# Query and key projections of three attention slots as seven block products instead of eight, in fp16, woven with attention; keys and values of two slots parked in HBM

## The chip, the cores and the metric

One Trainium2 chip, eight cores in two dies (cores 0 to 3 and 4 to 7), one program on all eight, each core with 1024 of the 8192 tokens. The metric is the device time of the slowest core in microseconds (us). Most fast executions of a kernel agree within 0.3%; some executions fall into a slower state in which the cores of one die are granted a lower clock (the kernel before, in one run: 2862.85 us, with a mean clock of 0.858 to 0.867 on cores 0 to 3 and 0.995 to 0.997 on the others). Every length of a stage below comes from a profiled execution whose eight cores were undisturbed, unless said.

Names: PE is the matrix engine, PEld its weight load, DVE the vector engine, ACT the scalar engine, POOL the general one, SP an engine that here issues transfers (`spdma`). SBUF holds the kernel's tiles, PSUM the results of its matmuls: the program declares it as eight banks of 128 x 512 fp32 (`psall`). DMA moves the weights and the parked tiles between HBM and SBUF.

## The reference, cut to what matters

A two-layer decoder trunk. Only the token mixer of the first layer is touched: dilated causal attention with 12 heads, in 3 groups by (window, dilation), 4 head slots each; a slot's three outputs are merged by their softmax denominators.

```python
ATTN_GROUPS = ((128, 1), (512, 4), (2048, 16))  # (window, dilation)

def _dilated_attention_mixer(h, positions, w_in):
    proj = h @ w_in                                # (B, S, 3*1536 + 512)
    q, k, v, q_mem = jnp.split(proj, [...], axis=-1)
    q = _partial_rotary(q..., positions)           # on 32 of the 128 head dims
    k = _partial_rotary(k..., positions)
    for g, (window, dilation) in enumerate(ATTN_GROUPS):
        o, l = _dilated_group(q[g], k[g], v[g], window, dilation)
    w = jax.nn.softmax(jnp.stack(lses, axis=0), axis=0)
    merged = jnp.einsum('gbsh,gbshd->bshd', w, jnp.stack(outs, axis=0))

# layer: x = x + concat([mix_out, mem_out]) @ w_out ; x = x + swiglu(rms_norm(x))
```

The tokens of a residue class (position modulo the dilation) form a subsequence, so queries and keys have to be regrouped by class somewhere between the projection and the scores.

## The kernel before

All instructions are declared as operations with what they read and write. A list scheduler then fixes the order on each engine ahead of time, from its own estimates of durations, and places the semaphores. `pe`, `act`, `dve`, `spdma` declare an operation; `bank(b)` is a PSUM bank, `PB(b)` its name for the dependencies.

The queries and keys of slot `s` are 6 column blocks (x = 0, 1 and u = 0 to 2) by two halves of tokens; each is 16 matmuls into one of two banks. The columns are permuted so that the 32 rotary rows of three heads share the block u = 0 and can be rotated at once.

```python
    OB = (0, 1)
    def qk_units(s):
        qk = QK[s % 2]
        def unit(x, u, th):
            def f():
                pc, c = divmod(x * 3 + u, 2)
                w = weights(("qk", s, pc), w0[W0_S + s * 3 + pc])
                b = nextbank(OB)
                proj(b, 512, [(lambda t, k=k: t.matmul(
                    bank(b), w[k * 256 + c * 128:k * 256 + c * 128 + 128], hT[k * TOK + th * 512:k * TOK + th * 512 + 512],
                    start=(k == 0), stop=(k == 15))) for k in range(16)], ...)
                # tile(i): the place of row i in QK, by residue class; st is the dilation
                if u == 0:
                    put[x, th] = rotary(b, 6 + th, 96)     # 3 DVE operations, 96 x 512
                    copy(2, 3, 1)                          # ACT, 32 rows
                    return
                copy(u - 1, None, 0)                       # ACT, 128 rows
                copy(2, 0, u + 1)                          # ACT, 32 rows
                put[x, th](u - 1, *tile(u - 1))            # DVE, 32 rotated rows
                if u == 2:
                    put[x, th](2, *tile(2))
```

The regrouping by class is a strided read, written in order:

```python
    def classes(ap, st):
        return ap if st == 1 else ap.rearrange("p (m r) -> p r m", r=st)

    def put(j, dst, dreg, st):                             # inside rotary
        dve(lambda v: v.tensor_tensor(out=dst[0:32], in0=classes(ta.ap[qs, 0:n], st), in1=classes(tb.ap[qs, 0:n], st), op=ALU.add), ...)

    def copy_rows(b, n, src, dst, dreg, to, st):
        if src is None:
            act(lambda a: a.copy(out=dst, in_=classes(bank(b)[:, 0:n], st)), [PB(b)], dreg, n)
        else:
            act(lambda a: a.copy(out=dst[32 * to:32 * to + 32], in_=classes(bank(b)[32 * src:32 * src + 32, 0:n], st)), [PB(b)], dreg, n)
```

A slot's attention is twelve batches: scores into bank 2 or 3, Exp on ACT, the mask on DVE, then values and denominators accumulated in banks 4 to 7. At its end ("the close") ACT takes Ln and Exp of the denominators and DVE multiplies. The slots and the output projection:

```python
    for s in range(4):
        ...
        attend(s)
        if s < 3:
            for f in qk_units(s + 1):
                f()

    def oproj0(t, j):          # 7 of 8 matmuls need only slots 0 to 2 and the memory heads
        for h in range(2):
            ks = ((4, 5, 6, 7, 0, 1, 2), (3,))[h]
            pe(mm[0:7] if h == 0 else mm[7:8], ...)
        add_x(b, t, j)
```

The softmax here doesn't subtract the row's maximum and nothing guards it: scores larger than these inputs give would overflow.

## Time and profile before

| | before |
|---|---|
| time, median of 3 runs | 2526.04 us (2524.78 to 2857.17) |
| first score of the memory heads ("start") | 347.2 us |
| from there to the last query or key product ("stage") | 162.1 us |
| from there to slot 3's result ("attn3") | 19.5 us |
| from there to the first matmul of the feed-forward ("oproj") | 59.45 us |
| from there to its first down projection ("ffn") | 535.4 us |
| the rest | 1393.6 us |

The start is the mean over the eight cores of one profiled execution, since its cores differ by up to 7 us (343.5 to 350.6 us here); the other stages are medians over the cores (so they need not add up exactly). The profiled core that the page shows is core 4. More views of it. First the whole stage as one row (window; busy us and count of PE, PEld, DVE, ACT, POOL; granted clock; DMA share; GB/s):

```profile
350.60:512.90 162.30, 159.76 (x1201) 86.10 (x1222) 80.74 (x132) 87.75 (x194) 4.75 (x9) 1.00 0.34 67
```

PE is idle 2.5 us of 162.3. The list of what PE waits for from 350 to 513 us (total us, times, longest):

```profile
PE psall L1094 <- DVE pm L1085: 1.1, 2, 0.7
PE psall L859 <- ACT QK L588: 0.3, 1, 0.3
```

And ACT's copies of query and key rows, by shape (count; busy us, mean ns; idle before and its releaser):

```profile
L588 ACT CAST QK<-psall 32x512 bf16<-32x512 f32 x35 | 20.1, 575 | 11.2 <-DVE t L572 10.2
L586 ACT CAST QK<-psall 128x512 bf16<-128x512 f32 x23 | 13.4, 583 | 35.2 <-PE psall L859 32.5 <-remote 2.7
```

Their mean is nearly the same for 32 and for 128 rows (575 and 583 ns) and, although most of them read every 4th, 8th or 16th element, no single one in the timeline is longer than 0.6 us.

### The profile page before, as it was taken

How to read it: one execution, taken by the hardware profiler on the slowest of the kernel's cores; microseconds unless marked ns; L12 is line 12 of the kernel's file. 1: busy time of each engine (PE TensorE's matmuls, PEld its weight loads, DVE VectorE, ACT ScalarE, POOL GpSimd, SP SyncE). 2: the span in 40 equal slices, each digit the busy share in tenths (PEclk: the TensorE clock that was granted, in tenths of full speed). 3: DMA queues.
4: the chain of work that ended last, by engine and by line, in shares of the span. 5: the costliest groups of instructions: out<-in, count | busy, mean ns of one | idle time of the engine just before them, and what ended most of it. 6: DMA issues, size and time to landing. Idle time of an engine off the chain costs nothing.

```text
span 2524.4 us, 38262 instructions; the slowest of 8 cores (2512.0 to 2524.4 us)
## 1 busy us (share of the span) xinstructions
PE 2459.5 (97%) x13993; PEld 1305.3 (52%) x14059; DVE 1549.7 (61%) x2716; ACT 839.9 (33%) x1464; POOL 148.7 (6%) x250
## 2 busy tenths in 40 slices
PE   7999999989999999999999999999999999999998
PEld 3454445544456666644444764444566666544443
DVE  4761425556456677657777766336676776567767
ACT  6762245454223333320003444134333333310004
POOL 1100000000000000000000000000000000000003
PEclk9999999999999999999999999999999999999999
DMA  9865754364876655797652443524756555786554
GB/s 160 130 102 84 138 102 78 68 184 94 184 128 136 126 104 112 139 212 155 132 126 52 84 85 77 106 73 88 167 103 140 115 106 115 183 189 133 126 132 150
DMA packets 73431, 310.28 MB, mean 123 GB/s; under 512 B 6688, under 2 KB 34848, under 8 KB 47520
## 3 DMA queue, kind: packets, MB, share of 16 engines
q0 software_dynamic: 37344, 218.36, 49.9%
q1 hardware_dynamic: 35904, 89.47, 10.3%
q8 instruction: 115, 1.88, 0.3%
q14 instruction: 68, 0.56, 0.1%
HBM read 482.65 MB, written 43.52 MB: 208 GB/s over the span
## 4 chain that ended last, share of the span: by engine, by line
PE 88%; DMA 4%; ACT 2%; DVE 2%; issue 2%; another core or an unknown queue 0%; POOL 0%; DVEq 0%; ACTq 0%; POOLq 0%
PE psall L1471 28%; PE psall L1678 20%; PE psall L1413 11%; PE psall L859 6%; PE psall L2127 4%; PE psall L2033 4%; PE psall L812 3%; PE psall L1873 3%; PE psall L775 2%; PE psall L1253 2%; PE psall L739 2%; DMA stg<-xT 1%; PE psall L896 1%; DMA fr<-wgu 1%; DMA b_B<-wd 1%
## 5 line engine op out<-in xcount | busy, mean ns | idle before, releaser
L1167 DVE TENSOR_TENSOR xs<-psall,xs 128x512 f32<-128x512 f32 x400 | 270.2, 687 | 210.0 <-PE psall L1678 134.5
L1471 PE MATMUL psall<-Sq,ft 128*128 128x512 f16 x1408 | 323.5, 379 | 0.0
L1678 PE MATMUL psall<-b_B,units 128*128 128x512 f16 x1408 | 315.4, 380 | 4.1 <-DMA b_B<-wd 2.9
L1477 ACT COPY snap<-psall 128x512 f32<-128x512 f32 x264 | 151.5, 586 | 299.4 <-PE psall L1471 222.6
L1678 PE MATMUL psall<-b_T,units 128*128 128x512 f16 x1056 | 237.4, 379 | 1.7 <-DVE xs L1167 1.0
L1678 PEld LDWEIGHTS psall<-b_B,units 128*128 128x128 f16 x1408 | 137.7, 98 | 171.0 <-issue 7.9
L1471 PE MATMUL psall<-hTq,ft 128*128 128x512 f16 x912 | 212.1, 381 | 2.3 <-DVE hTq L1243 2.3
L1471 PEld LDWEIGHTS psall<-Sq,ft 128*128 128x128 f16 x1408 | 137.4, 98 | 147.1 <-issue 0.8
L1173 ACT ACTIVATE junkB<-xs 128x1024 bf16<-128x1024 f32 x24 | 25.3, 1054 | 464.1 <-DVE xs L1167 463.0
L859 PE MATMUL psall<-hT,ring 128*128 128x512 bf16 x741 | 169.8, 379 | 2.2 <-ACT QK L588 0.8
L1678 PEld LDWEIGHTS psall<-b_T,units 128*128 128x128 f16 x1056 | 102.9, 98 | 126.1 <-issue 3.1
L1471 PE MATMUL psall<-Sq,fr 128*128 128x512 f16 x704 | 159.8, 379 | 0.3 <-DVE snap L1516 0.2
L1471 PEld LDWEIGHTS psall<-hTq,ft 128*128 128x128 f16 x912 | 89.5, 98 | 99.6 <-issue 4.4
L1516 DVE TENSOR_TENSOR snap<-psall,snap 128x512 f32<-128x512 f32 x88 | 60.4, 686 | 115.3 <-PE psall L1471 115.3
L859 PEld LDWEIGHTS psall<-hT,ring 128*128 128x128 bf16 x768 | 73.6, 98 | 84.5 <-issue 4.4
L2127 PE MATMUL psall<-ring,G 128*128 128x512 f16 x512 | 111.8, 379 | 1.4 <-DVE G L2057 1.4
L1471 PEld LDWEIGHTS psall<-Sq,fr 128*128 128x128 f16 x704 | 68.3, 98 | 83.3 <-issue 3.6
L1361 DVE TENSOR_TENSOR ft<-fr 128x2048 f16<-128x2048 f16 x88 | 106.8, 1216 | 4.7 <-DMA fr<-wgu 4.7
L1413 PE MATMUL psall<-a2f,t2w 128*128 128x256 f16 x744 | 106.4, 272 | 0.3 <-DVE psall L1429 0.2
L1335 POOL DMA_DIRECT2D fr<-wgu x88 | 46.5, 529 | 1016.3 <-PE psall L1471 813.6
L1482 ACT ACTIVATE sgb<-psall 128x512 f16<-128x512 f32 x88 | 52.4, 595 | 139.9 <-PE psall L1471 135.2
L1422 ACT COPY psall<-psall 128x512 f32<-128x512 f32 x93 | 53.2, 572 | 135.4 <-PE psall L1413 135.4
(255 smaller groups left out, 3728.5 us busy)
## 6 DMA issues: line engine op xcount, KB each, us to landing
fr<-wgu POOLq DMA_DIRECT2D x88, 1024.0 KB, 13.3
ring<-w POOLq DMA_DIRECT2D x38, 1024.0 KB, 9.9
b_B<-wd POOLq DMA_DIRECT2D x32, 896.0 KB, 10.9
hid<-fs SPq DMA_DIRECT2D x44, 512.0 KB, 10.5
b_B<-wd POOLq DMA_DIRECT2D x16, 1024.0 KB, 14.5
units<-hid SPq DMA_DIRECT2D x16, 896.0 KB, 8.1
ring<-wo POOLq DMA_DIRECT2D x12, 1024.0 KB, 9.4
stg<-xT POOLq DMA_DIRECT2D x20, 512.0 KB, 16.7
```

Source lines behind the costliest of these rows:

```text
L812: pe([(lambda t, k=k, hf=hf: t.matmul(bank(b), own_tile(hT[k * TOK:(k + 1) * TOK], gi, j), ws[hf][(k % 8) * 512:(k % 8 + 1) * 512], start= ...
L859: proj(b, 512, [(lambda t, k=k: t.matmul(bank(b), w[k * 256 + c * 128:k * 256 + c * 128 + 128], hT[k * TOK + th * 512:k * TOK + th * 512 + ...
L1167: dve(lambda v: v.tensor_tensor(out=xa, in0=bank(b), in1=xa, op=ALU.add), [PB(b), xr], [xr], 512)
L1361: dve(lambda v: v.tensor_tensor(out=T[0:2048], in0=w[1024:3072], in1=w[0:2048], op=ALU.subtract), [w.r(0, 3072)], [T.r(0, 2048)], 2048, 2)
L1413: pe([(lambda t, k=k: t.matmul(bank(b)[:, h * 256:(h + 1) * 256], W[:, k * 128:(k + 1) * 128], g_(k), start=(first and k == 0), stop=False ...
L1471: pe([(lambda t, k=k: t.matmul(bank(b), W[blk * 1024 + k * 128:blk * 1024 + k * 128 + 128], f(k), start=(first and k == 0), stop=(last and ...
L1477: act(lambda a: a.copy(out=s_.ap, in_=bank(b)), [PB(b)], [s_.r()], 512)
L1516: dve(lambda v: v.tensor_tensor(out=s7.ap, in0=bank(X), in1=s7.ap, op=ALU.add), [PB(X), s7.r()], [s7.r()], 512)
L1678: pe([(lambda t, k=k: t.matmul(bank(b), f(u, k), w[k * 512:(k + 1) * 512], start=(first and k == 0), stop=(last and k == hG - 1), skip_gro ...
L1873: pe([(lambda e, k=k, i=i, t=t: e.matmul(bank(b)[:, i * 256:(i + 1) * 256], f(k, t), w(k), start=(first and i == 0 and k == 0), stop=(last ...
L2033: pe([(lambda t, k=k: t.matmul(bank(b), W[blk * 1024 + k * 128:blk * 1024 + k * 128 + 128], f(k), start=(first and k == 0), stop=(last and ...
L2127: pe([(lambda t_, k=k, hh=hh, hf=hf: t_.matmul(bank(b), G1[t * 2048 + (hh * 8 + k) * 128:t * 2048 + (hh * 8 + k) * 128 + 128], ws[hh][k * ...
```

## The change

The intent: multiply the 2 x 2 blocks of activations and weights with seven products instead of eight (Winograd's form of Strassen's scheme), as the feed-forward of this kernel already does, for slots 1 to 3. That needs sums of activation blocks (made in place, once), sums of weight blocks (per piece of 256 columns), and PSUM results that are partly copied out ("snapshots", fp32, in SBUF) and added to later results. The operands become fp16. To make room, halo keys and values of slots 2 and 3 and the values of two slots wait in HBM and come back when slots 0 and 1 are done. Attention batches are woven between the products, and part of the output projection is put early into slot 3's attention.

```diff
@@ the source of the copies and of rotary is now a parameter: a bank or a snapshot
-    def copy_rows(b, n, src, dst, dreg, to, st):
+    def copy_rows(ap, sr, n, src, dst, dreg, to, st):
         if src is None:
-            act(lambda a: a.copy(out=dst, in_=classes(bank(b)[:, 0:n], st)), [PB(b)], dreg, n)
+            act(lambda a: a.copy(out=dst, in_=classes(ap[:, 0:n], st)), [sr], dreg, n)
@@ seven products
+    def qk_piece(s, pc, out):
+        X, Y = OB[pc_i[0] % 2], OB[1 - pc_i[0] % 2]
+        def sums():                  # T1, T2, T4: one 128x2048, two 128x1024 on DVE
+            ...
+        def snapshot(key, b):
+            s_ = st[key] = snq[sq2_i[0] % 5]
+            act(lambda a: a.copy(out=s_.ap, in_=bank(b)), [PB(b)], [s_.r()], 512)
+        def done(c, th, b, key=None):
+            x, u = divmod(pc * 2 + c, 3)
+            if key is None:
+                out(x, u, th, bank(b), PB(b))
+            else:
+                s_ = st[key]
+                dve(lambda v: v.tensor_tensor(out=s_.ap, in0=bank(b), in1=s_.ap, op=ALU.add), ...)
+                out(x, u, th, s_.ap, s_.r())
+        def f1(): prod(X, True, 0, A(0, 0), True, False);  snapshot("s1", X)
+        def f2(): prod(Y, True, 3, A(1, 0), True, True);   done(0, 0, Y, "s1")
+        def f3(): prod(X, False, 2, S(1), False, False);   snapshot("s2", X)
+        def f4(): prod(Y, False, 1, A(0, 1), True, False); snapshot("s7", Y)
+        def f5(): prod(X, False, 0, S(0), False, False);   done(1, 1, X, "s7")
+        def f6(): prod(Y, False, 3, A(1, 1), False, True); done(0, 1, Y, "s2")
+        def f7(): prod(X, True, 2, S(2), False, True);     done(1, 0, X)
@@ parking, ahead of the memory keys
+    spdma(lambda q: q.dma_start(out=kvx, in_=KVh[4 * HALO:8 * HALO]), ...)       # 2.75 MB
+    spdma(lambda q: q.dma_start(out=vox, in_=Vo[6144:12288]), ...)               # 1.57 MB
@@ weaving
-        attend(s)
+        parts, close = attend(s)
         if s < 3:
-            for f in qk_units(s + 1):
-                f()
+            todo = ...               # three pieces of seven products, and their weight sums
+            interleave(todo, parts)
+        else:
+            run(parts)
+        close()
+        if s < 2:
+            ...                      # bring back what was parked
@@ output projection
+    EARLY = [(0, 0), (0, 1), (4, 0), (4, 1), (1, 0)]
+    for t, j in EARLY:
+        oproj0(t, j, (4, 5, 6, 7, 0, 1, 2), OB)
```

Left out: the buffers, the place of each weight piece, the order of weight columns on the host, the sums of activations, and the same change of parameter in `rotary`.

## The prediction

Its sum: -15.5 + 4 + 2 + 1 - 1.5 = -10 us, from 2526 to 2516, shaded to 2515. The 1 us of parking and the 3 us of the wait for an output weight, part of the -1.5, are estimates.

> **What bounds the kernel now.** I read the page's busy shares, then the table by stage, then the timeline of the matrix engine between 350 and 600 us, and last the tables for DMA. Busy shares of the page:
>
> ```profile
> PE 2459.5 (97%) x13993; PEld 1305.3 (52%) x14059; DVE 1549.7 (61%) x2716; ACT 839.9 (33%) x1464; POOL 148.7 (6%) x250
> ```
>
> PE is the bound over the whole span. The change touches the first 600 us, so what counts is whether PE is the bound there. Table by stage (us; busy of PE, PEld, DVE, ACT, POOL; granted clock; DMA share; GB/s):
>
> ```profile
> 350.00:400.00 50.00, 49.63 (x383) 27.09 (x389) 24.68 (x43) 36.30 (x80) 1.58 (x3) 1.00 0.28 52
> 400.00:450.00 50.00, 49.20 (x379) 26.71 (x385) 25.68 (x43) 23.78 (x55) 2.11 (x4) 1.00 0.45 84
> 450.00:500.00 50.00, 48.68 (x375) 26.35 (x381) 24.96 (x41) 23.43 (x54) 1.06 (x2) 1.00 0.36 72
> ```
>
> From 350 to 500 us (memory attention, attention of slots 0 to 2, query and key products of slots 1 to 3) PE is 98% busy, DVE half, DMA a third. A matmul less there is time less, and DVE seems to have 25 us free in 50. The groups of instructions between 340 and 600 us give the work and its prices:
>
> ```profile
> L859 PE MATMUL psall<-hT,ring 128*128 128x512 bf16 x554 | 127.9, 379 | 1.4 <-ACT QK L588 0.3
> L579 DVE TENSOR_TENSOR QK<-t,t 32x512 bf16<-32x512 f32 x36 | 35.6, 988 | 38.7 <-ACT QK L586 38.4
> L1085 DVE TENSOR_TENSOR pm<-pt,masks 128x512 bf16<-128x512 bf16 x48 | 19.8, 422 | 23.0 <-ACT pt L1079 19.2 <-PE psall L1096 3.4
> L571 DVE STREAM_SHUFFLE t<-psall 96x512 f32<-96x512 f32 x12 | 8.7, 728 | 0.1
> ```
>
> The projection matmul (554 records of 576) waits 1.4 us in all. Its 379 ns is a latency; the pitch is in the timeline of PE:
>
> ```profile
> 302.23 13.98 PE L859 MATMUL psall<-hT,ring 128*128 128x512 bf16 x62
> 316.04 13.98 PE L896 MATMUL psall<-hT,ring 128*128 128x512 bf16 x63
> ```
>
> The 64 matmuls of a block (62 recorded) take 316.04 - 302.23 = 13.81 us, 0.2158 us each. After the products attention of slot 3 stands alone; table by stage:
>
> ```profile
> 515.00:520.00 5.00, 4.32 (x52) 2.78 (x51) 2.62 (x5) 2.06 (x6) 0.53 (x1) 1.00 0.60 206
> 520.00:525.00 5.00, 3.40 (x71) 2.70 (x66) 1.20 (x3) 4.56 (x19) 0.00 (x0) 1.00 0.94 185
> 525.00:530.00 5.00, 4.53 (x62) 2.84 (x62) 0.92 (x3) 0.70 (x2) 0.00 (x0) 1.00 0.23 84
> 530.00:535.00 5.00, 1.46 (x4) 0.48 (x5) 2.09 (x3) 1.98 (x2) 0.53 (x1) 0.87 1.00 324
> 535.00:540.00 5.00, 4.78 (x19) 2.09 (x20) 2.17 (x5) 4.06 (x9) 0.00 (x0) 0.78 1.07 279
> ```
>
> From 515 to 535 us PE is idle 0.68 + 1.60 + 0.47 + 3.54 = 6.3 us, and DMA becomes full. And one earlier place, where DMA is the limit already:
>
> ```profile
> 265.00:270.00 5.00, 5.00 (x25) 2.25 (x23) 0.00 (x0) 0.58 (x1) 0.53 (x1) 1.00 0.98 172
> 270.00:275.00 5.00, 3.80 (x17) 1.40 (x15) 3.72 (x8) 1.16 (x2) 0.00 (x0) 1.00 1.02 241
> 275.00:280.00 5.00, 3.75 (x26) 2.54 (x27) 0.00 (x0) 0.40 (x2) 0.00 (x0) 1.00 1.03 175
> ```
>
> There PE loses 2.5 us, 1.9 of it to weights of the memory keys.
>
> [...] the fp16 feed-forward matmuls show the same 379 ns. [...] 128x2048 fp16 takes 1216 ns, 128x1024 683 ns, 128x512 with a PSUM operand 687 ns. [...]
>
> **The change part by part.**
>
> *Products.* A slot has 2 token halves x 6 column blocks x 16 contraction blocks = 192 matmuls; as seven products, 3 pieces x 7 x 8 = 168. Three slots save 72 x 0.2158 = 15.5 us of PE, on the path.
>
> *Sums.* Prices from the feed-forward, which does the same: own sums 8 x 1.216 = 9.7 us; weight sums 9 x (1.216 + 2 x 0.683) = 23.2; additions to a snapshot 27 x 0.687 = 18.5: DVE gains 51.4 us. ACT gains 27 snapshots x 0.586 = 15.8, harmless. Rotary now mostly reads SBUF instead of PSUM[...] (676 and 679 ns): no change.
>
> Is DVE still hidden? Per slot before: 12 x 0.984 + 4 x (0.728 + 0.676 + 0.679) + 12 x 0.422 + 1.22 = 26.4 us. The change adds 7.7 + 6.2: 40.3. PE per slot: 36.3 of products and, by columns, 36 x 0.2158 = 7.8 of attention: 44.0. By durations DVE would be 92% full. Operations back to back start about 0.07 us earlier than durations say (a 0.68 us one followed after 0.60), 55 x 0.07 = 3.9 us, so some 36.4, 83%. Six of the eight own sums are placed before the memory attention, when DVE idles. PE stays the bound, narrowly.
>
> *Two banks.* Seven products of 8 matmuls (1.73 us each) alternate between two PSUM banks, and five times per piece the next but one product needs a bank that ACT or DVE has just read: DVE for second, fifth and sixth product. DVE has 1.73 us, plus some 0.4 us of attention, for an operation of 0.69 us behind whatever of up to 1.2 us is running. At 83% load I put 0.15 us on each of the 27 DVE hand-overs: 4 us back. This is judged, not measured.
>
> *Start.* The place of a piece's weights changes, and the first piece now loads last of three, at a point where DMA is full; one sum over the activations and the first weight sums can only start when the last memory query product is done. 2 us back.
>
> *Parking.* 2.75 MB of keys and values and 1.57 MB of values go out at about 260 to 285 us, and as much comes back, after slots 0 and 1. The return lies where the DMA share is 0.28 to 0.45: free. The way out meets full DMA[...]. The instruction order moves the memory keys' matmuls later (64 projection matmuls before them now, 40 before), which hides part. 1 us back.
>
> *Tail.* Before, four partial output projections of 7 matmuls fill the lone attention of slot 3; the instruction order now shows seven, 3 x 1.5 = 4.5 us of the 6.3 idle. But one output weight, loaded long ahead before, now shares full DMA with another and with 2 MB of residual rows; the last two partials need those and stand ahead of the last attention products in PE's order. 9.4 us is the median for one alone[...]. I put 3 us on that wait: net -1.5.
>
> Everything later is untouched. Sum: -15.5 + 4 + 2 + 1 - 1.5 = -10 us. From 2526: 2516, which I shade to 2515.
>
> **The rivals.** *Full gain:* no new waits and a filled tail, -15.5 - 4.5 = -20, 2506. For it: DVE stands at half, and the feed-forward runs the same scheme at PE 98% or more. Against it: that has six banks, not two, and no attention in between. *DVE becomes the bound:* if operations overlap less than I take, or its fixed order puts 2.8 us of rotary ahead of an addition for which PE waits, a slot takes 47 to 49 us rather than 44; almost all of 49.3 is back, and the time is 2522 to 2527. For it: 92% by durations. Against it: the order shows additions between rotary steps. *DMA takes the gain:* parking delays memory and query weights before 350 us, and the two output weights hold PE at the tail; each could cost 5 us more: 2525. For it: a share of 1.0 in both places. Against it: the loads are ordered early and the stage before 350 has slack between 280 and 300 us.
>
> **Range and chances.** Full gain is the floor, DVE as the bound near the ceiling; I give the middle most: 2508 to 2525, 8 in 10. 2% is 50 us; the change reaches only 160 us and saves 15 of them at best, so "within 2%" is close to certain. Slower by 2% would need a stall of 60 us; nothing suggests one, but reordering could bring one.
>
> **What would show it.** Products right: 504 matmuls of this kind instead of 576, pitch still 0.216. DVE: about 40 us per 50 in that stage, and PE waits for snapshot additions or copies of 3 to 6 us in all; under 1 us means full gain, over 10 DVE as the bound. Start: PE idle by about 2 us around 350 to 357. Parking: PE waits for weights between 260 and 350 us of no more than 4 us. Tail: idle of PE between the last product and the final output projection below 6 us, with a wait for an output weight. Everything after must keep its length within 1 us. Wrong would be: a stage from 350 us to slot 3's attention that shortens by under 5 or over 15 us, or a changed clock with fp16 activations.

## The result, and the profile after

| | before | after |
|---|---|---|
| median | 2525.41 us (2524.46 to 2857.17, 4 runs) | 2523.28 us (2522.22 to 2585.27, 4 runs) |
| ratio | | 0.9991, 95% 0.9972 to 1.0011 |

A ratio is the mean time of one kernel's fast runs over that of the other's of the same rounds, so it is not quite the ratio of the medians. The change is correct. By the run times alone it is not told from no change, since the interval holds 1; by the stages it is worth about 2 us, where 10 were forecast: inside the range of the prediction, but its sum was wrong. Where it went, by stage (the start and the last row are means over the cores, the others medians):

| stage | before | after | difference | forecast |
|---|---|---|---|---|
| start | 347.2 | 349.3 | +2.1 | +3 (start and parking) |
| stage | 162.1 | 158.1 | -4.0 | -15.5 + 4 = -11.5 |
| attn3 | 19.5 | 23.9 | +4.4 | } -1.5 |
| oproj | 59.45 | 55.75 | -3.7 | } |
| ffn | 535.4 | 535.55 | +0.15 | 0 |
| rest | 1393.6 | 1394.0 | +0.4 | 0 |
| first matmul of the feed-forward, mean | 588.7 | 586.7 | -2.0 | |

The last row agrees with the medians of the run times, so the answer lies in the first 590 us. The page's profiled core of the kernel after is core 1; below I use core 4 of the same execution, as before (its span is 2513.4 us, the longest of the eight 2520.6: its start came earlier, its stages have the lengths of the others).

Page, busy shares (core 1):

```profile
PE 2450.1 (97%) x13987; PEld 1297.9 (51%) x13987; DVE 1599.5 (63%) x2783; ACT 873.8 (35%) x1491; POOL 148.7 (6%) x250
```

PE's work went down by 9.4 us, DVE's up by 49.8 and ACT's by 33.9. Table by stage of core 4, the three 50-us windows of the prediction and then the stage as one row:

```profile
350.00:400.00 50.00, 48.35 (x353) 25.54 (x351) 34.52 (x59) 41.60 (x83) 1.06 (x2) 1.00 0.24 44
400.00:450.00 50.00, 45.98 (x380) 24.66 (x379) 37.42 (x60) 34.42 (x62) 1.58 (x3) 1.00 0.47 109
450.00:500.00 50.00, 45.69 (x348) 23.80 (x347) 37.71 (x60) 34.75 (x63) 2.11 (x4) 1.00 0.56 131
```

```profile
346.30:504.60 158.30, 147.23 (x1137) 77.62 (x1136) 115.49 (x183) 117.86 (x218) 4.75 (x9) 1.00 0.43 95
```

PE is busy 12.5 us less and idle 11.1 instead of 2.5 us. (Why 12.5, when the products alone save 15.5: by its columns at the pitch of 0.216 us the stage holds some 158.8 us of matmuls before and 142.7 after, an estimate. The busy times show 1.0 and 4.5 us more than that: a matmul shows 379 ns where the pitch is 216, and so can hide short waits behind it; no run separated them.) DVE, the suspect of the prediction, has 36.5 us of work per 50, less than the 40 it reckoned with. ACT has 30.1 us more, twice the 15.8 it reckoned with. What PE waits for in the stage:

```profile
PE psall L947 <- DVE snq L962: 3.0, 2, 1.6
PE psall L947 <- ACT QK L592: 2.7, 5, 1.1
PE psall L1173 <- ACT pt L1188: 2.2, 3, 0.9
PE psall L947 <- ACT snq L954: 1.2, 2, 0.7
PE psall L1125 <- ACT pt L1123: 1.1, 2, 0.9
PE psall L1173 <- DVE QK L583: 0.8, 1, 0.8
```

L947 is a product, L1173 a score of a slot. Three of the four largest are ACT's. The copies of L592 that end the waits of products read PSUM, since a copy from SBUF frees no bank; in the timeline four of the five stand directly behind slow copies in ACT's fixed order (at 410 us behind two of 1.14 and 1.15 us). Its groups in the stage:

```profile
L592 ACT CAST QK<-snq 32x512 bf16<-32x512 f32 x27 | 29.4, 1090 | 11.6 <-DVE snq L962 11.1
L590 ACT CAST QK<-snq 128x512 bf16<-128x512 f32 x18 | 17.0, 947 | 14.7 <-DVE snq L962 14.7
L954 ACT COPY snq<-psall 128x512 f32<-128x512 f32 x27 | 15.9, 588 | 6.3 <-PE psall L947 6.0
...
L592 ACT CAST QK<-psall 32x512 bf16<-32x512 f32 x9 | 5.2, 575 | 1.0 <-DVE t L576 0.8
```

The snapshots (L954) cost what was forecast, 15.9 us. The rest is a copy that no one added: 45 row copies, 39 of them with a stride, now read a sum in SBUF (`snq`) instead of a bank, and the same 32x512 copy that takes 575 ns from PSUM takes 1090 ns from there. In the 128-row group the mean mixes two kinds: in the timeline, those without a stride take 0.61 to 0.68 us and those with one 1.06 to 1.14.

How a late ACT copy becomes idle PE shows in one gap, 403 to 408 us. Timelines of ACT, DVE and PE (start us, length us, engine, instruction; in brackets the idle time before it and what ended it):

```profile
402.90 1.08 ACT L590 CAST QK<-snq 128x512 bf16<-128x512 f32 x1
404.01 1.11 ACT L592 CAST QK<-snq 32x512 bf16<-32x512 f32 x1
```

```profile
404.08 2.21 DVE L583 TENSOR_TENSOR QK<-t,t 32x512 bf16<-32x512 f32 x2 [0.50 <-ACT QK L590]
406.31 0.69 DVE L962 TENSOR_TENSOR snq<-psall,snq 128x512 f32<-128x512 f32 x1
```

```profile
403.65 1.03 PE L947 MATMUL psall<-Sa,ring 128*128 128x512 f16 x4
404.52 0.38 PE L1173 MATMUL psall<-QK 128*128 128x256 bf16 x2
404.74 1.03 PE L947 MATMUL psall<-Sa,ring 128*128 128x512 f16 x4
407.14 1.89 PE L947 MATMUL psall<-hT,ring 128*128 128x512 f16 x8 [1.38 <-DVE snq L962]
```

ACT's strided copy ends at 403.98. DVE's put, which fills rows of the same tile, waited 0.50 us for it; the addition that frees the bank stands behind two puts in DVE's fixed order and ends at 407.0; PE, whose next product needs that bank, waits 1.38 us. The copy explains 0.50 of it; the two puts, 2.21 us, were there before the change. The first two PE rows also give the pitch: four products in 404.52 - 403.65 = 0.87 us, 0.217 each, as before.

The start: the PE waits of core 4 from 200 to 346 us contain one for the last weight piece of slot 0's queries and keys, where before there was 1.9 us for memory keys' weights:

```profile
PE psall L899 <- DMA ring<-w: 3.2, 1, 3.2
```

The tail, table by stage and timeline of PE:

```profile
505.00:510.00 5.00, 2.51 (x18) 1.23 (x17) 4.91 (x6) 4.92 (x7) 0.00 (x0) 0.80 0.73 211
510.00:515.00 5.00, 5.00 (x49) 3.29 (x48) 3.23 (x6) 1.48 (x5) 0.53 (x1) 0.86 0.49 75
...
525.00:530.00 5.00, 2.77 (x28) 1.36 (x27) 1.23 (x1) 2.08 (x2) 0.00 (x0) 1.00 1.01 415
```

```profile
507.69 0.19 PE L1203 MATMUL psall<-pm,KVh 128*128 128x64 bf16 x1 [2.49 <-DVE attnT L1255]
```

The filling works: PE is full from 510 to 525 (the rows left out read 5.00 too). Most of attn3's +4.4 us is this filling itself: 49 matmuls of partial output projections in place of 28, an estimate of 4.5 us at the pitch, work that oproj then lacks. So attn3 and oproj are best read together, +0.7. But a new wait of 2.5 us stands ahead of it: slot 3's first value matmul overwrites the accumulators of slot 2, which are free only when slot 2's close is done. The multiplication that ends slot 2's close, in the timeline of DVE before and after:

```profile
481.09 1.22 DVE L1142 TENSOR_TENSOR attnT<-psall,rden 128x1024 bf16<-128x1024 f32 x1 [3.36 <-ACT rden L1139]
```

```profile
506.33 1.21 DVE L1255 TENSOR_TENSOR attnT<-psall,rden 128x1024 bf16<-128x1024 f32 x1
```

Before, it came 32 us ahead of the last product (512.9) and was hidden; woven over all of the products, it comes 1.7 us after the last one (504.6). Behind the wait stands something that the prediction had no term for: the rows of 505 to 515 us show a granted clock of 0.80 and 0.86, and the first partial output projection after the wait takes 3.17 us where the next one, of as many matmuls, takes 1.67 (core 4).

### The profile page after: what moved, and what is told of

It reads as the page before. It is cut to its first block, busy times and chain, and to the rows that moved or that the text cites. A ratio compares the mean times of both kernels' runs of the same rounds, so it can differ in the third digit from the quotient of the medians.

```text
span 2520.6 us, 38404 instructions; the slowest of 8 cores (2512.6 to 2520.6 us)
## 1 busy us (share of the span) xinstructions
PE 2450.1 (97%) x13987; PEld 1297.9 (51%) x13987; DVE 1599.5 (63%) x2783; ACT 873.8 (35%) x1491; POOL 148.7 (6%) x250
## 4 chain that ended last, share of the span: by engine, by line
PE 86%; DMA 5%; DVE 3%; ACT 3%; issue 2%; POOL 0%; DVEq 0%; ACTq 0%; POOLq 0%
PE psall L1605 29%; PE psall L1812 20%; PE psall L1547 11%; PE psall L2261 4%; PE psall L2167 4%; PE psall L947 3%; PE psall L2007 3%; PE psall L816 2%; PE psall L1383 2%; PE psall L779 2%; DMA ring<-w 1%; DMA hT<-xT 1%; PE psall L743 1%; PE psall L899 1%; PE psall L1000 1%
## 5 line engine op out<-in xcount | busy, mean ns | idle before, releaser
L1568 DVE TENSOR_TENSOR psall<-psall,s5b 128x256 f32<-128x256 f32 x93 | 40.2, 433 | 88.1 <-PE psall L1547 88.1
L1605 PE MATMUL psall<-hTq,fr 128*128 128x512 f16 x416 | 93.2, 380 | 2.0 <-DVE upb L1637 1.0
```

The source lines that it names most:

```text
L1605: pe([(lambda t, k=k: t.matmul(bank(b), W[blk * 1024 + k * 128:blk * 1024 + k * 128 + 128], f(k), start=(first and k == 0), stop=(last and ...
```

## The experiments

Theories for the missing time, which the runs were chosen to tell apart: (A) ACT's row copies from SBUF are slow and hold up the chain; (B) two banks for seven products are too few; (C) DVE's own added work is; (D) parking or the load order delays the start; (E) weaving costs, by the exposed close. Eighteen kernels ran. Stages, in us. "Sum" is stage + attn3 + oproj. The start and the last column are means over the cores, the others medians.

| kernel | start | stage | attn3 | oproj | sum | first ffn matmul |
|---|---|---|---|---|---|---|
| before | 347.2 | 162.1 | 19.5 | 59.45 | 241.05 | 588.7 |
| after | 349.3 | 158.1 | 23.9 | 55.75 | 237.75 | 586.7 |
| e1_plain_copies | 349.5 | 152.8 | 22.9 | 55.75 | 231.45 | 581.0 |
| e2_no_weave | 349.0 | 165.6 | 21.5 | 56.95 | 244.05 | 592.9 |
| e3_close_early | 351.1 | 158.4 | 21.5 | 56.65 | 236.55 | 587.8 |
| e4_park_only | 346.4 | 162.1 | 19.5 | 59.45 | 241.05 | 587.7 |
| e5_early_off (disturbed) | 354.7 | 158.1 | 23.4 | 61.15 | 242.65 | 597.9 |
| e6_third_bank | 348.9 | 151.0 | 27.05 | 55.5 | 233.55 | 583.0 |
| e7_third_inplace | 349.5 | 150.5 | 26.8 | 55.5 | 232.8 | 582.4 |
| e8_best | 349.4 | 158.0 | 24.55 | 55.9 | 238.45 | 587.9 |
| e9_load_order | 348.6 | 160.2 | 23.9 | 55.25 | 239.35 | 587.6 |
| e10_fp16_only | 346.5 | 162.1 | 19.45 | 60.35 | 241.9 | 588.1 |
| e11_strided_write | 349.0 | 206.7 | 27.8 | 55.9 | 290.4 | 638.8 |
| e12_write_and_puts | 348.8 | 216.85 | 31.6 | 55.5 | 303.95 | 653.5 |
| e13_late_park | 347.1 | 158.0 | 24.0 | 55.7 | 237.7 | 584.3 |
| e14_no_weight_sums | 350.5 | 156.1 | 28.6 | 55.15 | 239.85 | 589.9 |
| e15_combined | 347.4 | 153.4 | 23.35 | 56.35 | 233.1 | 581.1 |
| e16_plain_third | 349.9 | 146.3 | 26.75 | 55.5 | 228.55 | 578.2 |
| e17_third_late | 348.4 | 150.5 | 26.85 | 55.5 | 232.85 | 581.2 |
| e18_all_psum | 348.0 | 151.0 | 25.6 | 54.1 | 230.7 | 578.8 |

### A: the copies

**e1_plain_copies.** Wrong result: row copies from SBUF read their source in order. Nothing else changes, not even the order of instructions, because the scheduler's estimate of a copy doesn't depend on its stride.

```diff
     def copy_rows(ap, sr, n, src, dst, dreg, to, st):
+        if sr[0] == "S" and st > 1:      # source in SBUF
+            ... in_=ap[:, 0:n].rearrange("p (r m) -> p r m", r=st) ...   # same shape, in order
+            return
```

> Changed kernel, but the row copies that read a sum in SBUF read it in order instead of regrouped by class (wrong result on purpose; same instructions in the same order). In the changed kernel these copies take 1.09 us on ACT against 0.58 us from PSUM. If the slow copies are what holds the matrix engine (they hold ACT, and DVE waits for them before it frees a bank), they fall to about 0.6 us, idle of PE between the first memory score and the last product falls from 11 us to under 6, and that stage from 158.1 us to 151 to 154. If it is the two banks and DVE's load, the stage stays within 157 to 158.5 although the copies are faster.

ACT's groups from SBUF in this run:

```profile
L592 ACT CAST QK<-snq 32x512 bf16<-32x512 f32 x27 | 16.6, 616 | 13.1 <-DVE snq L968 12.6
```

1090 ns became 616. The stage went from 158.1 to 152.8, and the sum fell by 6.3 us; the runs agree: 2518.75 us (2515.74 to 2563.22), ratio to before 0.9975 (0.9953 to 0.9997). Theory A is shown: the stride of the copies alone costs 6.3 us of the sum (5.7 at the first feed-forward matmul).

**e11_strided_write and e12_write_and_puts.** The obvious remedy: read in order and put the stride on the write side, for ACT's copies (e11) and for DVE's puts as well (e12). Both correct.

```diff
+        if sr[0] == "S" and st > 1:
+            i_, o_ = ap.rearrange("p (m r) -> p m r", r=st), dst.rearrange("p r m -> p m r")
+            act(lambda a: a.copy(out=o_, in_=i_), [sr], dreg, n)      # the 32-row case is left out
+            return
```

> Changed kernel, but the row copies from SBUF sums walk the sum in order and write the bf16 rows with the stride, in place of reading with the stride and writing in order; result stays correct. If reading fp32 with a stride from SBUF is what doubles the copy (1.09 us), it falls to 0.6 to 0.7 us, the stage from 158.1 to about 153 us as in the run with plain copies, and the total by 5 to 6 us. If any strided SBUF access costs the same, copies stay at 1.05 us or more and the stage at 158.

> As the previous kernel, and the 36 rotary additions on DVE (0.98 us mean, 1.05 strided, 0.68 in order) write with the stride too. If the write stride is free on DVE also, they fall to 0.68 us, DVE in the stage from 116 to about 106 us, and the stage by up to another 1 to 3 us (150 to 153). If not, no change against the previous kernel.

A clear miss. ACT's copies in e11, then DVE's puts in e12:

```profile
L594 ACT CAST QK<-snq 32x512 bf16<-32x512 f32 x19 | 47.2, 2482 | 9.9 <-DVE snq L970 9.5
```

```profile
L586 DVE TENSOR_TENSOR QK<-t,t 32x512 bf16<-32x512 f32 x20 | 48.6, 2430 | 17.2 <-ACT QK L599 14.8 <-ACT QK L603 2.0
```

This bf16 write of 32x512 with a stride takes 2.48 us on ACT and 2.43 on DVE, more than twice the fp32 read with a stride (1.09 on ACT in the kernel after, 1.01 to 1.08 on DVE in the kernel before). The stage grew by 48.6 and 58.8 us (ratios to before 1.0195, 1.0175 to 1.0215, and 1.0261, 1.0244 to 1.0279). No remedy, but good evidence for A: with the order of instructions unchanged, copies of 0.62, 1.09 and 2.48 us gave stages of 152.8, 158.1 and 206.7.

**e10_fp16_only.** The kernel before with only activations and weights in fp16.

```diff
-    hT = sb("hT", 64 * KB, 32 * KB)
+    hT = sb("hT", 64 * KB, 32 * KB, F16)
```

> Kernel before with activations, staging and projection weights in fp16 instead of bf16 and nothing else of the change. Tests whether fp16 itself costs: expected are the lengths of the kernel before (162.1, 19.5, 59.5 us, pitch 0.216) and a clock of 0.994 to 0.997. The first memory score came 2.1 us later in the changed kernel; if fp16 causes it, it shows here (349 instead of 347 us); if it stays at 346 to 347.5 us, fp16 is not the cause.

Stage 162.1 against 162.1, 2525.74 us (2524.64 to 2545.59), ratio 1.0027 (0.9987 to 1.0068): fp16 itself costs nothing that these runs can see; the projection matmul's median is 379 ns, as in bf16.

### B: the banks

**e6_third_bank.** The middle products of a piece (f4 and f6) get a bank of their own, taken from the scores, which keep one bank until slot 3.

```diff
-        X, Y = OB[pc_i[0] % 2], OB[1 - pc_i[0] % 2]
+        X, Y, V = GRP[pc_i[0]]           # (0,1,1), (1,3,0), then (y,v,x) of the last
-            prod(Y, False, 1, A(0, 1), True, False);  snapshot("s7", Y)
+            prod(V, False, 1, A(0, 1), True, False);  snapshot("s7", V)
-            prod(Y, False, 3, A(1, 1), False, True);  done(0, 1, Y, "s2")
+            prod(V, False, 3, A(1, 1), False, True);  done(0, 1, V, "s2")
-            sb_ = nextbank((2, 3))
+            sb_ = nextbank((2,) if s < 3 else (2, 3))
```

> Changed kernel, the seven products rotate over three PSUM banks (attention scores keep one bank instead of two while products run); sums still go to SBUF and are copied from there at 1.09 us. If the two-bank hand-over is the larger cause of the 11 us of PE idle in the stage, the stage falls from 158.1 to 151 to 154 us. If the slow copies load ACT and DVE as such (as the run with plain copies says, 152.8 us), a third bank only delays the wait: 155 to 158 us. A single score bank could cost up to 3 us.

The stage shortens by 7.1, to 151.0, but attn3 grows by 3.15: with one score bank 21 more of slot 2's attention matmuls are left after the last product (an estimate of 0.9 us), and a score waits 2.3 us for an Exp there. Net, 4.2 us of the sum. Four runs from 2520.7 to 2522.96 us; the kernel before ran only slow on that chip, so there is no ratio. **e7_third_inplace** adds the sums in PSUM for the first column block of a piece, so that 30 of the 45 copies read a bank again:

```diff
+                if c == 0:
+                    dve(lambda v: v.tensor_tensor(out=bank(b), in0=bank(b), in1=s_.ap, op=ALU.add), ...)
+                    out(x, u, th, bank(b), PB(b))
+                    return
```

> As the three-bank kernel, and two of three sums are added in place in PSUM, so that rotary and row copies read PSUM: copies at 0.58 us again for 18 of 27 sums, at the price of a bank held longer. Correct result. If slow strided copies are the cause and the third bank pays for the longer hold: stage 150 to 154 us, ACT busy in it from 118 to about 105 us, total 4 to 7 us lower than the changed kernel. If holding banks longer costs more than the copies gain: stage over 156 us.

Sum 232.8, only 0.75 less than e6: the copies that still read SBUF, or the longer hold on the bank, eat the rest. Its two fast runs are 2520.89 and 2522.43 us.

**e16_plain_third.** e1 and e6 together (wrong, as e1).

> Three banks and plain copies together (wrong result on purpose). Stage plus slot 3's attention is 182.0 us in the changed kernel, 175.7 with plain copies, 178.1 with three banks. If the two are separate causes, the sum is 172 to 173.5 us; if the third bank only helps against slow copies, it is 175 to 176.

Stage 146.3, sum 228.55: 9.2 us below the kernel after, where e1 alone gave 6.3 and e6 alone 4.2. So the two causes are separate and nearly add up. What PE of core 4 still waits for in the stage:

```profile
PE psall L1135 <- ACT pt L1133: 1.1, 2, 0.9
PE psall L1213 <- DVE pm L1204: 0.7, 2, 0.4
```

Both are waits of attention: no product waits for a hand-over any more, on any of the eight cores. And the stage is now where full gain would put it, 162.1 - 15.5 = 146.6, though it is helped by some 1.5 us of attention (an estimate by columns) that has moved behind its end. What is still missing of the 15.5 us is in the tail: attn3 and oproj together are 82.25 us against 78.95 before. Ratio to before 0.9954 (0.9904 to 1.0004).

### C: DVE's added work

**e14_no_weight_sums.** Weight sums only for the first piece (wrong), which takes 8 x 2.6 = 21 us from DVE.

```diff
-            for lo, n, a, ar, b, br in ((0, 2048, ...
+            for lo, n, a, ar, b, br in () if (s, pc) != (1, 0) else ((0, 2048, ...
```

> Changed kernel with the weight sums made for the first piece only (wrong result on purpose): DVE loses 20.7 of the 51 us that the change gave it, copies stay slow. If DVE's load is a separate cause of the stage's idle time, the stage falls from 158.1 to 154 to 156 us. If it is ACT and the banks, it stays over 157 us.

Inconclusive. The stage is 2.0 shorter and attn3 4.7 longer (with one wait of 5.4 us for an Exp), because the scheduler made another order. By this run C is neither shown nor excluded. What speaks against it is e16: DVE has the same work there (114.7 us in the stage of core 4 against 115.5), and no product waits for it. Its part in the waits of the kernel after, beside slow copies and two banks, stays open.

### D: the start

**e4_park_only.** The kernel before with two stores of the same sizes at the same place in the program.

```diff
+    spdma(lambda q: q.dma_start(out=kvx, in_=Vh.ap), [Vh.r(), KTh.r()], [kreg("kvx")], "kvx", 1.37)
+    spdma(lambda q: q.dma_start(out=vox, in_=Vo[6144:12288]), [Vo.r(6144, 12288)], [kreg("vox")], "vox", 0.78)
```

> Kernel before plus only the two stores of the parking (2.75 and 1.57 MB to HBM, read by nobody), at the place where the change has them. If the way out of the parking delays loads of weights, the first memory score comes 1 to 4 us later than in the kernel before (347.2 us as mean of eight cores) and the rest keeps its lengths (162.1, 19.7, 59.7 us); total +1 to +4 us. If the 2.1 us later start of the changed kernel has another cause (fp16, order), nothing moves by over 0.5 us.

Start 346.4, no delay (fast runs 2523.25 and 2526.0, ratio 0.9999). In the old layout that part of the values is complete earlier, so the store went out earlier (on core 4 before 225 us, where the kernel after issues it at 260.2). It wasn't the same test.

**e9_load_order.** The kernel after with the old order of places for the weight pieces, the other suspect.

```diff
-            ("qk", 1): (120, 112, 104), ("qk", 2): (120, 112, 104), ("qk", 3): (120, 112, 104)}
+            ("qk", 1): (112, 120, 104), ("qk", 2): (112, 120, 104), ("qk", 3): (112, 120, 104)}
```

> Changed kernel with the three weight pieces of a slot placed so that the first piece loads first (places as slot 1 had before). Tests the start: PE waits 1.1 us in memory attention before the first product weights are there. If the order of loads matters, the first 20 us lose that wait and the stage falls by 1 us; the first memory score stays at 349.3 us. If nothing moves, the order of loads was no cause. The output weight in the first place then comes later by a piece, which could lengthen the time after the last product by 0 to 2 us.

Start 348.6, at the edge of the scatter of the kernels that park as the change does (348.8 to 349.9 in nine undisturbed ones, 350.5 and 351.1 in two); the stage is 2.1 longer. A miss, and not the cause.

**e13_late_park.** The value store also waits until slot 0's third weight piece has landed.

```diff
-    ... [Vo.r(6144, 12288)], [kreg("vox")], "vox", 0.78)
+    ... [Vo.r(6144, 12288), weights(("qk", 0, 2), w0[W0_S + 2]).r()], [kreg("vox")], "vox", 0.78)
```

> Changed kernel; the store of the values to HBM (1.57 MB) waits until the third weight piece of slot 0's products has landed. In the changed kernel PE waits 3.2 us for that piece, at about 295 us, with DMA full. If the store causes it, the wait falls below 1 us and the first memory score comes at 346 to 347.5 us rather than 349.3, the rest unchanged (the stage may gain up to 1 us if the sums that overwrite the values' place start later). If the keys' store alone is enough, the wait stays above 2 us.

Start 347.1, as before the change (347.1 to 348.4 in the four kernels that have this edit). Of the two waits of core 4's PE at that product in the same stretch, the one for weights (3.2 us) is gone and this one is left:

```profile
PE psall L899 <- ACT QK L592: 0.5, 1, 0.5
```

Over the eight cores PE waits for transfers 1.8 to 3.5 us (mean 2.5) from 200 to 343 us in the kernel after, and 0 to 1.6 (mean 0.3) here; before the change the mean is 0.7. Parking's way out is shown as the cause of that wait, and with it of most of the +2.1 us at the start. The one dependency is no full cure: in e15, e17 and e18, which have it too, three or four of the eight cores still wait 1.9 to 3.1 us (means 0.8, 1.0 and 1.2), and why is open. Fast runs 2521.85 and 2521.26 us.

### E: weaving and the tail

**e2_no_weave.** Attention of a slot, its close, then the products.

```diff
-            interleave(todo, parts)
+            run(parts)
+            close()
+            run(todo)
```

> Changed kernel with the program order of before: all of a slot's attention first, its close, then the three pieces of the next slot (the scheduler still fills). If weaving costs by delaying the close of slot 2, the 2.5 us wait for its result at the start of slot 3's attention goes, and the time from the last product to the end of slot 3's attention falls from 23.8 to about 21 us. If weaving is needed to hide the two-bank hand-over, the stage up to the last product grows from 158 to over 160 us. Both may be true; then the total is within 3 us of the changed kernel.

Stage 165.6, longer than before the change, while attn3 falls to 21.5, as expected; 2531.33 us (2529.34 to 2752.75), ratio 1.0023 (1.0 to 1.0046). PE's waits on hand-overs of the products (for additions, row copies and snapshots) are 7.1 us here against 6.9, and those of attention, which now runs without products beside it, come on top: 2.1 us for the rotated rows, 1.8 for Exp, 1.0 for masks (0.8, 2.2 and none in the kernel after). Some 2 us more are attention of slot 2 that now ends inside the stage (671 of its matmuls in place of 631, an estimate by columns). The sum is 6.3 us longer, so weaving is needed; the waits listed explain only a part of it, and the total is not within 3 us of the kernel after, as was expected.

**e3_close_early.** All attention of a slot woven into its first 16 of about 24 steps, then the close, then the rest.

```diff
-            interleave(todo, parts)
+            interleave(todo[0:16], parts)
+            close()
+            run(todo[16:])
```

> Changed kernel with each slot's attention woven into the first two of its three pieces and closed before the third. Expected if the late close is a cause: 23.8 us from last product to end of attention becomes 21 to 21.5; the stage up to the last product stays at 158 +- 1; total 2 to 2.5 us lower than the changed kernel. If the third piece alone then stalls on its two banks, the stage grows by 1 to 4 us and eats it.

attn3 falls by 2.4 us, and the wait for slot 2's close is gone: that slot 2 ends late is shown as its cause. The edit doesn't separate the close from the last of slot 2's attention, 40 matmuls (an estimate of 2.1 us) that now end inside the stage too. But oproj grew by 0.9 and the feed-forward by 2.4 (537.9), the start by 1.8; the time is 2525.09 us (2520.61 to 2991.25), ratio 0.9987 (0.9958 to 1.0016), no gain. Why the feed-forward grew stays open. **e8_best**, a third bank with in-place sums and the early close, was meant to collect all gains:

> As the three-bank kernel with sums in place, and each slot's attention closed before its third piece. Expected, if both causes are additive: stage as that kernel within 1.5 us, last product to end of slot 3's attention 21.5 us instead of 23.9, total 5 to 9 us lower than the changed kernel and 7 to 11 below the kernel before.

It lost the third bank's: stage 158.0. PE waits 4.2 us for row copies and 3.4 us for Exp of the slots; batches pressed into two thirds of the stage stand closer together, and the last products stand alone. Which of the two costs more was not separated.

**e5_early_off.** No early partial output projections (`EARLY = []`).

> Changed kernel without the five early partial output projections placed in slot 3's attention (all as in the kernel before). If they fill idle time, the time from last product to the end of slot 3's attention falls by less than the output projection grows: 23.9 falls to 20 to 22 us, 55.8 grows to 59 or 60 us, the sum 79.6 grows by 1 to 3 us. If they only move work, the sum stays at 79.6 +- 0.5 us.

attn3 23.4 and oproj 61.15, that is 4.9 us more of the two together: the filling of the tail does work, by more than the 1 to 3 us expected. Two cores of this profile (2 and 3) were granted 0.984 of the clock; the six others give 84.0 to 85.8 us for the two stages, so the result doesn't hang on them.

### Versions that gain

**e15_combined** is e7 with the late parking and, for slot 2 only, an early close after 20 steps.

> Correct kernel: three banks with sums in place, late store of the values, and only slot 2's attention closed a few products earlier. If causes add up: first memory score 347 us, stage 150 to 152 us, last product to end of slot 3's attention 23 to 25 us instead of 26.8, total 2513 to 2517 us, 4 to 9 us below the changed kernel. If the early close with one score bank stalls the stage again, it is over 154 us.

2519.83 us (2517.71 to 2918.23), ratio 0.9964 (0.9935 to 0.9994). attn3 falls to 23.35 but the stage gives 2.9 back, so the 2513 to 2517 expected were missed. **e17_third_late** is the same without the early close:

> Three banks with two of three sums in place, and the late store of the values; no early close. From parts: first memory score 347.2, stage 150.5, slot 3's attention 26.8, output projection 55.5: first feed-forward matmul at 580.2 us (586.7 changed, 588.7 before), total 6 to 7 us under the changed kernel.

2519.52 us (2517.93 to 2702.5), ratio 0.9982 (0.9936 to 1.0027), sum 232.85 as e7, and less than the 6 to 7 us expected below the kernel after.

**e18_all_psum** is e17 with the third sum of a piece written into the free bank Y, so that row copies read PSUM (all but two of the first piece). It is correct.

```diff
+                o_ = b if c == 0 else Y
+                if c == 0 or Y != V:
+                    dve(lambda v: v.tensor_tensor(out=bank(o_), in0=bank(b), in1=s_.ap, op=ALU.add), ..., [PB(o_)], 512)
+                    out(x, u, th, bank(o_), PB(o_))
+                    return
```

> As the kernel beside it, and the third sum goes to the bank that is free then, so that of 45 slow copies only some 2 to 4 of the first piece still read SBUF. Correct result. If the slow copies are all that separates it from the wrong-result kernel with three banks and plain copies (stage plus slot 3's attention 173.1 us), the sum falls from 177.3 to 173 to 175 us and the first feed-forward matmul comes at 576 to 578 us, total 9 to 11 us under the changed kernel. If holding the extra bank costs, it stays at 177 or above.

ACT's copies of 32 and of 128 rows:

```profile
L592 ACT CAST QK<-psall 32x512 bf16<-32x512 f32 x35 | 20.1, 575 | 8.9 <-DVE t L576 6.0 <-DVE QK L583 2.3
...
L590 ACT CAST QK<-psall 128x512 bf16<-128x512 f32 x23 | 13.6, 590 | 15.2 <-DVE psall L968 14.5 <-PE psall L951 0.5
```

All of these are back at their price of before. Yet the stage and attn3 together are 176.6 us, where 173 to 175 were expected if the slow copies were all that separates this kernel from e16: the stage is no shorter than e17's (151.0 against 150.5), and on core 4 its products still wait 2.6 us for hand-overs, so what e18 gains lies in attn3 and oproj. Holding a bank longer is the likely price, not shown by itself. 2516.41 us (2515.12 to 2536.5) against 2526.25 for the kernel before on that chip; the first feed-forward matmul comes at 578.8 instead of 588.7. The ratio of fast runs, 0.9978 (0.9937 to 1.0019), doesn't exclude 1 by itself: two of its six fast runs had two cores at 0.984 of the clock and took 2536 us, the other four 2515.1 to 2516.8. The stages on eight cores (sum 230.7 against 241.05, 10.35 less) are what this rests on. It is the best correct version: 10 us below before, 7 below after.

## Why the prediction was right or wrong, point by point

The prediction named as a sign of being wrong a stage that shortens by under 5 us, and it shortened by 4.0. The measured time also lies in the range that it gave to its rival "DVE becomes the bound" (2522 to 2527), but that is luck: DVE isn't the bound, as the points below show. (A slip of the prediction: it calls full gain, 2506, the floor, and starts its range at 2508.)

- **Products: right.** 504 matmuls of this kind (144 + 144 + 144 + 72), pitch 0.217 us, no cost of fp16 (e10). In e16 the stage shows the whole 15.5 us, the sum 12.5.
- **ACT: this step failed.** "ACT gains 27 snapshots x 0.586 = 15.8, harmless", together with "Rotary now mostly reads SBUF instead of PSUM ... no change". ACT gained 30.1 us: the snapshots' 15.9, and longer copies, by durations 29.4 + 17.0 less (27 x 0.575 + 18 x 0.583), that is 20.4 (records of operations back to back overlap, on core 4 one of 0.63 us at 361.09 and the next at 361.63, so busy time shows less than their sum). And it was not harmless: 6.3 us of time (e1). The second sentence looked at the rotary's own operations, which read in order, and at DVE only; it is true of them (672 to 679 ns). The operations that changed source and have a stride are ACT's copies, and they were not priced at all. The prediction's own profile held the hint: L579, a put of 512 columns that reads fp32 from SBUF by class, takes 988 ns, where an operation of the rotary that reads as many columns in order is priced at 679 in its text. That mean is a mix: 30 of the 36 puts read with a stride and take 1.01 to 1.08 us, the six in order 0.68. The stride cost these reads from SBUF 0.33 to 0.40 us each even before the change.
- **Two banks: right in kind, and of about the size.** 4 us were put on it, "judged"; a third bank gives 7.1 in the stage, and 4.2 net of what the lost score bank costs in attn3 (e6). But the prediction laid all of PE's new waits on DVE hand-overs, and more than half of what PE waits for is ACT (2.7 + 2.2 + 1.2 + 1.1 of 11.0 us), and additions, snapshots and row copies together held products for 6.9 us, where 3 to 6 were forecast.
- **DVE: right that it is not the bound**, 36.5 us per 50 against 40 forecast; and in e16 no product waits for it. Its part in the waits of the kernel after was not isolated (e14).
- **Start and parking: right in sum, wrong in part.** +2.1 against "2" and "1". The wait sits at slot 0's third weight piece and is parking's (e13), which was to cost 1 us. Of the 2 us reckoned for weight order and sums, 1.1 us may be there, as waits for Exp near 348 us (core 4): the first product comes 3.8 us after the first memory score, where it came after 0.4 before, so nothing fills them. The load order isn't their cause (1.3 us of them with the old one, e9), and the sums were not tested.
- **Tail: failed.** Forecast -1.5, measured +0.7. Filling gives 3.7 us in oproj, but no wait for an output weight came; what came was a wait for slot 2's close, 2.5 us, the slower clock behind it (0.80 and 0.86), and 14 more attention matmuls behind the last product (an estimate of 0.6 us). That this wait is about as long as the 3 us put on the output weight is luck. The weaving was read for what it does to PE's gaps and not for when a slot's last batch now ends.
- **Everything later: right** within 0.6 us, and the mean clock of the cores did not change (0.994 to 0.997 before, 0.994 to 0.996 after).

In numbers: -11.5 forecast for the stage against -4.0, a miss of 7.5, of which e1 shows 5.3 in the stage; -1.5 against +0.7 in the tail. Both errors are of the same kind: an operation that keeps its name and count, and changes its price or its place. Still open: DVE's share in the waits; what a single score bank costs the tail (on core 4 of e18 a score waits 2.6 us there for an Exp, and values 1.7 for a mask); and why the feed-forward grew in e3.

## What to carry to other kernels

When a change moves the source of an operation from PSUM to SBUF, price that operation again with its access pattern, even if its count and shape stay: here 45 copies that nobody added took 20.4 us more of ACT, and the 27 that were added took 15.9. Ask of every woven schedule which buffer the next stage needs first and when its last user now ends. And when an algorithm saves on the busiest engine, its gain is what the hand-overs between products leave: with two banks and short products, 16 us saved became 2, with a third bank and sums kept in PSUM 10.
